# Later stores and weight loads, a fourth evacuation buffer, and a mask added later, in a hybrid decoder layer

## The chip, the cores and the metric

The kernel runs on one core of a Trainium2 chip. The metric is the device time of one execution in microseconds (us). All times below are us unless ns is written.

## What is computed

One layer of a hybrid decoder trunk on a sequence of 1024 rows of 1024 channels, in float32. The rows are normalised, multiplied by one wide input matrix (`w_in`), and the columns of the product feed four mixers of 256 channels each. Cut to what matters here:

```python
h = rms_norm(x, norm_w[i])
c = split_columns(h @ w_in[i])
y_nsa  = nsa_mixer(...)        # sparse attention: compressed, selected and window branch
y_diff = diff_mixer(...)       # differential attention
y_ret  = retention_mixer(...)  # chunked recurrence, chunks of 128 rows
y_ssm  = ssd_mixer(...)        # chunked state-space scan, chunks of 128 rows
# each times silu of a gate column group, concatenated, @ w_out, + x, final rms_norm
```

In the scan (`ssd_mixer`) every chunk needs, for each head, the matrix `exp(cs_l - cs_s)` under a causal mask, multiplied elementwise by the product of C and B, and then products with the rows of x scaled by `dt`.

## The kernel before

Float32 products are made from two parts, a rounded high part and the rest as a low part, so each logical matmul of a projection is three matmuls: high by high, low by high, high by low (L266 to L268 where the weights are stationary, L282 to L284 where the activations are).

Three streams are traced as Python generators and merged by weights: `attention` (differential heads 0 to 3, then sparse heads 4 to 7), `recurrent` (the compression network, then 16 chunks: eight for each pair of heads, of the scan `ssd_group` and of the retention `ret_pair`, zipped), and `projections` (25 groups of weight columns, two more being traced before the merge; then the gates, the output products and the final norm). A scheduler then writes the order of each engine's instructions at build time, from their priorities and a model of their times; attention and recurrence are lifted by 500 places. On the chip an engine takes its list strictly from the head, and so does SP, which issues nearly all DMAs. An edge called NOSYNC binds only the order in that list: on the chip nothing waits for it.

A projection (`proj_t`, or `proj_n` with 256 columns) first loads its weights raw (`weights`, L249, two buffers `wraw`), rounds them on ScalarE (ACT, L253, `whi`), and subtracts on GpSimd (POOL, L186 through `low`, `wlo`). It accumulates in two PSUM banks `mm` over eight steps k, for two halves u of the rows, and an evacuation function per kind of column moves each half through ring `ev` (three buffers of 2 KB a partition) and stores it to DRAM, since the mixers read it in another layout: `evac_split` (two tiles, two stores through `move`, L298), `evac_conv` (convolution and SiLU on VectorE (DVE), store at L752), `evac_rqk`, `evac_rv`, `evac_cmp`, `evac_z`, `evac_zs`. Names put into the set `done` let another stream go on, once its inputs are stored. The ring `ev` also holds the gate rows that `gated` loads back (L1135) and multiplies (DVE, L1136), and the residual rows of `out_partial`.

In `ssd_group` a chunk goes like this: load of x, B, C (`ch`, L761), transposes and the product of B and C (L764 to L766), copy to `xb` (ACT, L768), rows scaled twice on POOL (L771, L772), two loads of the cumulative sums from `d_cs` spread over all partitions (L774 `seg`, L775 `csl`), the causal mask added to `csl` on POOL (L776), per head a sum on DVE (L779) and an exponential on ACT (L781), one product on DVE (L782), and then the matmuls L784, L785 and L787, where L787 needs the result of L782.

Of the kernel before, what the change touches and what calls it, by code (L numbers as in the profile page):

```python
# [11 lines left out]
F32 = mybir.dt.float32  # L12
# [3 lines left out]
ALU = mybir.AluOpType  # L16
# [20 lines left out]
LEAD = 3  # L37
AHEAD = 2
FREE = 8
LO_POOL = 5  # L40
# [82 lines left out]
def hybrid_trunk_kernel(ctx: ExitStack, tc: tile.TileContext, a, out, dbg=None):  # L123
# [5 lines left out]
    dram = ctx.enter_context(tc.tile_pool(name="dr", bufs=1, space=bass.MemoryType.DRAM))  # L129
    RINGS = dict(wraw=(2, 4352), whi=(2, 4352), wlo=(2, 4352), ev=(3, 2048), e=(4, 2048), pth=(3, 2048),  # L130
                 ptl=(3, 2048), t=(8, 1024), u=(4, 1024), sm=(8, 32), sj=(2, 576), ch=(3, 1536), ce=(3, 1024))
# [56 lines left out]
    def bc(ap, n):  # L188

        return ap[:, :, None].to_broadcast([ap.shape[0], ap.shape[1], n])  # L190
# [44 lines left out]


    w_in = a["w_in"][0].rearrange("(k p) c -> p k c", p=P)
    w_out = a["w_out"][0].rearrange("(k p) c -> p k c", p=P)

    def weights(w, cols):  # L240

        c = sum(n for _, n in cols)
        step = 8 if c <= 128 else 4
        parts = []
        for k0 in range(0, NK, step):
            raw = sb("wraw", [P, step, c])
            o = 0
            for off, n in cols:
                SP.dma_start(raw[:, :, o:o + n], w[:, k0:k0 + step, off:off + n])  # L249
                o += n  # L250
            hi = sb("whi", [P, step, c], F32R)
            lo = sb("wlo", [P, step, c], F32R)
            A.activation(hi, raw, AF.Copy)  # L253
            flat = [t_.rearrange("p k c -> p (k c)") for t_ in (lo, raw, hi)]
            low(*flat)
            parts.append((hi, lo))
        return [(parts[k // step][0][:, k % step, :], parts[k // step][1][:, k % step, :]) for k in range(NK)]

    def proj_t(cols, evac):

        w = weights(w_in, cols)
        for u in range(2):
            hs = slice(u * 512, u * 512 + 512)
            p = ps("mm", [P, 512])
            for k in range(NK):
                paced(T.matmul(p, w[k][0], h_hi[k][:, hs], start=(k == 0), stop=False))  # L266
                T.matmul(p, w[k][1], h_hi[k][:, hs], start=False, stop=False)  # L267
                T.matmul(p, w[k][0], h_lo[k][:, hs], start=False, stop=(k == NK - 1))  # L268
                if k < NK - 1:
                    yield  # L270
            evac(u, p)
            yield

    def proj_n(cols, evac, w=None, step=True):

        c = sum(n for _, n in cols)
        w = w or weights(w_in, cols)
        for t in range(NT):
            hs = slice(t * P, (t + 1) * P)
            p = ps("mm", [P, c])  # L280
            for k in range(NK):
                paced(T.matmul(p, h_hi[k][:, hs], w[k][0], start=(k == 0), stop=False))  # L282
                T.matmul(p, h_hi[k][:, hs], w[k][1], start=False, stop=False)  # L283
                T.matmul(p, h_lo[k][:, hs], w[k][0], start=False, stop=(k == NK - 1))  # L284
                if step and k % 2 and k < NK - 1:
                    yield
            evac(t, p)
            yield
# [8 lines left out]
    def move(dst, src):  # L297
        SP.dma_start(dst.bitcast(F32), src.bitcast(F32))  # L298
# [118 lines left out]
    def evac_split(store, j, scale=1.0):  # L417

        def f(u, p):
            hi, lo = sb("ev", [P, 512], F32R), sb("ev", [P, 512], F32R)  # L420
            split(hi, lo, p, scale)
            for i, e in enumerate((hi, lo)):
                move(store[i, j * P:(j + 1) * P, u * 512:u * 512 + 512], e)
        return f
# [310 lines left out]
    def evac_conv(i):  # L735
        tl = const("tl%d" % i, [P, 3])

        def f(u, p):
# [12 lines left out]
            V.scalar_tensor_tensor(acc, th, 1.0, acc, op0=ALU.add, op1=ALU.mult)  # L751
            SP.dma_start(d_conv[i, :, u * 512:u * 512 + 512], acc)  # L752
        return f

    def ssd_group(g):
        dt, da, dd = dtt[:, 0, :], dtt[:, 1, :], dtt[:, 2, :]
        for c in range(NT):
# [46 lines left out]
    def evac_rqk(i, j):  # L804
        def f(u, p):
            e = sb("ev", [P, 512])
            A.activation(e, p, AF.Copy)
            SP.dma_start(d_rqk[i, j, :, u * 512:u * 512 + 512], e)
        return f

    def evac_rv(t, p):
        e = sb("ev", [P, 256])
        A.activation(e, p, AF.Copy)
        SP.dma_start(d_rv[t * P:(t + 1) * P, :], e)

# [93 lines left out]
    def evac_cmp(u, p):  # L909
        ev = sb("ev", [P, 512])  # L910
        A.activation(ev, p, AF.Copy)
        SP.dma_start(d_kv[:, u * 512:u * 512 + 512], ev)

# [210 lines left out]
    def evac_z(ct):  # L1124
        def f(u, p):
            th = sb("ev", [P, 512])
            A.activation(th, p, AF.Tanh, scale=0.5)
            V.scalar_tensor_tensor(th, th, 1.0, p, op0=ALU.add, op1=ALU.mult)
            SP.dma_start(d_z[ct, :, u * 512:u * 512 + 512], th)
        return f  # L1130
# [14 lines left out]
    def evac_zs(t, p):  # L1145
        th = sb("ev", [P, 256])
        A.activation(th, p, AF.Tanh, scale=0.5)
        V.scalar_tensor_tensor(th, th, 1.0, p, op0=ALU.add, op1=ALU.mult)
        SP.dma_start(d_zs[t * P:(t + 1) * P, :], th)

# [137 lines left out]

    done = set()

# [4 lines left out]
    def projections():  # L1295
        run(ssd_prep())
        yield from pt("diff_q", 1, evac_split(d_dq, 1, 32.0 ** -0.5))
        yield from pt("diff_k", 1, evac_split(d_dk, 1))
        done.add("diff1")
# [6 lines left out]
        done.add("nsa")  # L1306
        yield from pt("xbc", 0, evac_conv(0))
# [4 lines left out]
        yield from proj_n([(OFF["ret_v"], 256)], evac_rv)  # L1312
        done.update(("conv0", "ret0"))
        yield from pt("xbc", 1, evac_conv(1))
# [3 lines left out]
        yield from pt("xbc", 5, evac_conv(5))  # L1318
        done.update(("conv1", "ret1"))
        yield from proj_n([(OFF["ssm_z"], 256)], evac_zs)  # L1320
        done.add("ssm_z")
        for ct, n in ((2, "diff_z"), (4, "ret_z"), (0, "nsa_z")):
            for j in range(2):
                yield from pt(n, j, evac_z(ct + j))
        w_out0 = out_weights(ORDER[0:2], 0)[0]
        free(*h_hi, *h_lo)
# [16 lines left out]
        yield from out_final()  # L1343

    proj = projections()
    done.add("diff0")

# [102 lines left out]
```

## Time and profile before

| | |
|---|---|
| median of 3 executions | 753.74 us (751.43 to 753.95) |
| profiled execution, its own time | 753.33 us |
| its span, first to last instruction | 751.4 us |
| TensorE (PE) busy | 710.7 us, 95% |
| VectorE (DVE) busy | 519.6 us, 69% |
| ScalarE (ACT) busy | 409.6 us, 55% |
| GpSimd (POOL) busy | 298.1 us, 40% |
| DMA engines | 105.96 MB, mean 141 GB/s |

The span is shorter than the execution's own time by 1.9 us, which lies around it. A busy share is a mean over stages: idle time of an engine matters only where PE ends up waiting for it.

### The profile page before, as it was taken

How to read it: one execution, taken by the hardware profiler on the slowest of the kernel's cores; microseconds unless marked ns; L12 is line 12 of the kernel's file. 1: busy time of each engine (PE TensorE's matmuls, PEld its weight loads, DVE VectorE, ACT ScalarE, POOL GpSimd, SP SyncE). 2: the span in 40 equal slices, each digit the busy share in tenths (PEclk: the TensorE clock that was granted, in tenths of full speed). 3: DMA queues.
4: the chain of work that ended last, by engine and by line, in shares of the span. 5: the costliest groups of instructions: out<-in, count | busy, mean ns of one | idle time of the engine just before them, and what ended most of it. 6: DMA issues, size and time to landing. Idle time of an engine off the chain costs nothing.

```text
span 751.4 us, 12303 instructions
## 1 busy us (share of the span) xinstructions
PE 710.7 (95%) x3796; PEld 587.6 (78%) x3796; DVE 519.6 (69%) x1493; ACT 409.6 (55%) x1022; POOL 298.1 (40%) x469
## 2 busy tenths in 40 slices
PE   4999999999999999989999999999989999999994
PEld 4988787768888898777899788688766878788773
DVE  4853466446976867778798957667789996345577
ACT  6722465556777656556575544554465853543343
POOL 4233128212132114442533544545577742632522
PEclk9999999999999999999999999999997999999998
DMA  8658826756722533536333723335374233431365
GB/s 295 186 156 240 225 85 179 209 164 178 204 73 89 142 102 92 129 87 179 106 101 98 188 87 84 91 102 134 104 206 127 68 102 129 140 126 60 126 252 196
DMA packets 103406, 105.96 MB, mean 141 GB/s; under 512 B 15747, under 2 KB 78797, under 8 KB 103325
## 3 DMA queue, kind: packets, MB, share of 16 engines
q1 hardware_dynamic: 103244, 104.82, 47.5%
q8 instruction: 30, 0.49, 0.3%
q14 instruction: 36, 0.29, 0.2%
q0 software_dynamic: 96, 0.36, 0.1%
HBM read 72.96 MB, written 32.54 MB: 140 GB/s over the span
## 4 chain that ended last, share of the span: by engine, by line
PE 68%; DVE 14%; DMA 8%; ACT 4%; issue 3%; POOL 2%; SPq 1%; POOLq 0%; DVEq 0%; ACTq 0%
PE mm L266 9%; PE mm L268 9%; PE mm L267 9%; PE S L172 7%; PE O L1106 3%; PE mm L282 3%; PE mm L283 3%; PE mm L284 3%; PE S L1087 2%; DMA t<-d_cs 2%; PE R L1211 1%; PE R L1212 1%; PE R L1213 1%; PE mm L1211 1%; PE S L1031 1%
## 5 line engine op out<-in xcount | busy, mean ns | idle before, releaser
L186 POOL TENSOR_TENSOR wlo<-wraw,whi 128x256 fp32r<-128x256 f32 x132 | 98.5, 777 | 161.8 <-ACT whi L253 148.4
L266 PE MATMUL mm<-h,whi 128*128 128x512 f32 x400 | 160.0, 401 | 0.8 <-ACT whi L253 0.4
L267 PE MATMUL mm<-h,wlo 128*128 128x512 f32 x400 | 159.2, 399 | 0.0
L268 PE MATMUL mm<-h,whi 128*128 128x512 f32 x400 | 159.1, 398 | 0.0
L476 ACT ACTIVATE S<-S,sj 128x512 f32<-128x512 f32 (+3 forms) x192 | 103.3, 538 | 83.2 <-DVE sj L475 61.1
L172 PE MATMUL S<-b,b 100*128 100x256 f32 (+5 forms) x384 | 133.4, 373 | 6.5 <-ACT e L632 2.7
L475 DVE CUSTOM_DVE_ANT_0 S<-S,mk 128x512 f32<-128x512 f32 (+3 forms) x144 | 70.2, 495 | 39.4 <-PE S L172 18.2
L172 PEld LDWEIGHTS S<-b,b 100*128 100x128 f32 (+1 forms) x384 | 72.5, 193 | 24.9 <-ACT S L476 6.6
L266 PEld LDWEIGHTS mm<-h,whi 128*128 128x128 f32 x400 | 75.9, 190 | 16.3 <-ACT whi L253 0.7
L268 PEld LDWEIGHTS mm<-h,whi 128*128 128x128 f32 x400 | 75.7, 189 | 16.4 <-issue 0.4
L267 PEld LDWEIGHTS mm<-h,wlo 128*128 128x128 f32 x400 | 75.9, 190 | 14.4
L1101 POOL TENSOR_SCALAR pth<-e 128x512 fp32r<-128x512 f32 (+2 forms) x64 | 41.4, 649 | 63.4 <-ACT e L1096 28.8
L1096 ACT ACTIVATE e<-S 128x512 f32<-128x512 f32 (+2 forms) x76 | 40.9, 541 | 31.9 <-PE S L1091 19.7
L1102 DVE TENSOR_TENSOR ptl<-e,pth 128x512 fp32r<-128x512 f32 (+2 forms) x64 | 44.9, 706 | 18.1 <-POOL pth L1101 14.2
L282 PE MATMUL mm<-whi,h 128*128 128x256 f32 (+1 forms) x192 | 55.5, 291 | 1.7 <-DVE ev L744 1.1
L283 PE MATMUL mm<-wlo,h 128*128 128x256 f32 (+1 forms) x192 | 55.5, 291 | 0.1
L284 PE MATMUL mm<-whi,h 128*128 128x256 f32 (+1 forms) x192 | 54.2, 288 | 0.0
L473 DVE TENSOR_REDUCE sj<-S 128x1 f32<-128x512 f32 x48 | 32.5, 683 | 17.0 <-PE S L172 10.4
L632 ACT ACTIVATE e<-S 128x512 f32<-128x512 f32 (+1 forms) x64 | 35.9, 568 | 13.6 <-PE S L172 8.2
L282 PEld LDWEIGHTS mm<-whi,h 128*128 128x128 f32 x192 | 36.7, 192 | 2.8 <-DVE ev L744 1.3
L283 PEld LDWEIGHTS mm<-wlo,h 128*128 128x128 f32 x192 | 36.7, 191 | 1.6 <-POOL wlo L186 0.7
L476 ACT ACTIVATION_READ_ACCUMULATOR S<-S,sj 128x1 f32 x192 | 37.6, 196 | 0.0
(321 smaller groups left out, 1652.5 us busy)
## 6 DMA issues: line engine op xcount, KB each, us to landing
wraw<-in_w_in_dram SPq DMA_DIRECT2D x27, 512.0 KB
b<-in_x_dram SPq DMA_DIRECT2D x8, 512.0 KB
t<-d_cs SPq DMA_DIRECT2D x32, 128.0 KB
wraw<-in_w_out_dram SPq DMA_DIRECT2D x16, 256.0 KB
ev<-in_x_dram SPq DMA_DIRECT2D x16, 256.0 KB
d_part<-ev SPq DMA_DIRECT2D x16, 256.0 KB
b<-d_part SPq DMA_DIRECT2D x8, 512.0 KB
out_dram<-b SPq DMA_DIRECT2D x16, 256.0 KB
```

The source lines that it names most:

```text
L172: ins = T.matmul(tile_, *args, **kw)
L186: G.tensor_tensor(dst[:, cs], src[:, cs], hi[:, cs].bitcast(F32), op=ALU.subtract)
L266: paced(T.matmul(p, w[k][0], h_hi[k][:, hs], start=(k == 0), stop=False))
L267: T.matmul(p, w[k][1], h_hi[k][:, hs], start=False, stop=False)
L268: T.matmul(p, w[k][0], h_lo[k][:, hs], start=False, stop=(k == NK - 1))
L282: paced(T.matmul(p, h_hi[k][:, hs], w[k][0], start=(k == 0), stop=False))
L283: T.matmul(p, h_hi[k][:, hs], w[k][1], start=False, stop=False)
L284: T.matmul(p, h_lo[k][:, hs], w[k][0], start=False, stop=(k == NK - 1))
L475: V.tensor_tensor_reduce(s, s, bound, -1.0, -NEG, ALU.add, ALU.min, nm)
L476: A.activation(s, s, AF.Exp, bias=nm, scale=1.0 if bound is None else -1.0, accum_out=self.d[:, b, i, c:c + 1])
L1101: G.tensor_scalar(hl[0], e, 1.0, 1.0, op0=ALU.mult, op1=ALU.mult)
L1102: V.tensor_tensor(hl[1], e, hl[0].bitcast(F32), op=ALU.subtract)
```

## The change

A store of an evacuated projection half is no longer issued where the evacuation is traced: `later` puts it on a list, and `tick`, called after every step k of a projection (every second one in `proj_n`), traces it three steps later, with an edge that puts it behind that step's matmul in the schedule. `mark` does the same with the names in `done`; `flush` traces what is left at the ends. The stores of `evac_n1` and `evac_nsa_v` stay where they were. A load of raw weights gets an edge to the matmul that ended the first half of the projection two before it (`halfway[-2]`). Ring `ev` has four buffers in place of three. In `ssd_group` the addition of the mask (L776 before) gets an edge that puts it behind the second row scaling (L772 before); both are on POOL.

```diff
+DEFER = 3
-    RINGS = dict(..., ev=(3, 2048), ...)
+    RINGS = dict(..., ev=(4, 2048), ...)
+    def later(dst, src):
+        deferred.append([lambda: SP.dma_start(dst, src), DEFER])
+
+    def tick(ins):
+        for d in deferred:
+            d[1] -= 1
+        while deferred and deferred[0][1] <= 0:
+            st = deferred.pop(0)[0]()
+            if st is not None:
+                tc.add_manual_dep(st.ins, ins.ins.name, NOSYNC, reason="later")
+
+    def mark(*names):
+        deferred.append([lambda: done.update(names), DEFER])
+
+    def flush():
+        while deferred:
+            deferred.pop(0)[0]()
...
-                SP.dma_start(raw[:, :, o:o + n], w[:, k0:k0 + step, off:off + n])
+                ins = SP.dma_start(raw[:, :, o:o + n], w[:, k0:k0 + step, off:off + n])
+                if len(halfway) > 2:
+                    tc.add_manual_dep(ins.ins, halfway[-2].ins.name, NOSYNC, reason="raw")
...
-                T.matmul(p, w[k][0], h_lo[k][:, hs], start=False, stop=(k == NK - 1))
+                ins = T.matmul(p, w[k][0], h_lo[k][:, hs], start=False, stop=(k == NK - 1))
+                tick(ins)
...
+            if u == 0:
+                halfway.append(ins)
...
-            SP.dma_start(d_conv[i, :, u * 512:u * 512 + 512], acc)
+            later(d_conv[i, :, u * 512:u * 512 + 512], acc)
...
-            G.tensor_tensor(xs[:, 1], xn, bc(dd[:, hc], 64), op=ALU.mult)
+            scaled = G.tensor_tensor(xs[:, 1], xn, bc(dd[:, hc], 64), op=ALU.mult)
...
-            G.tensor_tensor(csl, csl, pair(m_causal_t), op=ALU.add)
+            ins = G.tensor_tensor(csl, csl, pair(m_causal_t), op=ALU.add)
+            tc.add_manual_dep(ins.ins, scaled.ins.name, NOSYNC, reason="order")
...
-        done.add("cmp")
+        mark("cmp")
```

The other evacuation stores and the other names go through `later` and `mark` in the same way.

## Rows read from the trace of the kernel before

**Rows 1.** Page: busy us (share of the span) xinstructions of each engine.

```profile
PE 710.7 (95%) x3796; PEld 587.6 (78%) x3796; DVE 519.6 (69%) x1493; ACT 409.6 (55%) x1022; POOL 298.1 (40%) x469
```

**Rows 2.** Windows: stretch, length, busy of PE PEld DVE ACT POOL, clock, DMA.

```profile
25.00:725.00 700.00, 680.24 (x3637) 562.15 (x3638) 484.42 (x1413) 381.02 (x954) 279.66 (x440) 0.99 0.46 133
50.00:75.00 25.00, 25.00 (x112) 20.22 (x111) 11.29 (x33) 4.57 (x7) 7.00 (x10) 1.00 0.85 253
322.80:326.15 3.35, 3.35 (x9) 2.61 (x9) 3.23 (x11) 3.32 (x8) 1.57 (x4) 0.50 0.17 65
554.90:558.25 3.35, 3.35 (x12) 2.68 (x12) 3.25 (x13) 2.42 (x6) 2.37 (x4) 0.50 0.97 288
565.20:575.30 10.10, 9.99 (x29) 6.40 (x28) 10.07 (x29) 5.53 (x15) 7.48 (x11) 0.50 0.39 127
```

**Rows 3.** Waits of PE: who ended them, us in total, times, longest.

```profile
PE S L172 <- ACT e L632: 2.7, 1, 2.7
PE O L1106 <- POOL pth L1101: 2.5, 3, 1.4
...
PE S L172 <- ACT e L1096: 1.1, 1, 1.1
```

**Rows 4.** Waits of the other engines.

```profile
POOL t L776 <- DMA t<-d_cs: 39.5, 9, 16.8
DVE t L779 <- POOL t L776: 26.6, 13, 4.4
...
DVE ev L1136 <- DMA ev<-d_z: 7.4, 4, 2.6
```

**Rows 5.** Timelines of SP, POOL, DVE, ACT, PE, third chunk: start, us, instruction, [idle before].

```profile
310.51 0.33 SPq L752 DMA_DIRECT2D d_conv<-ev  x1
...
313.57 0.38 SPq L775 DMA_DIRECT2D t<-d_cs  x1
...
319.04 0.67 POOL L776 TENSOR_TENSOR t<-t,mk 128x256 f32<-128x256 f32 x1 [4.34 <-DMA d_ssm<-t]
...
319.74 0.93 DVE L779 SCALAR_TENSOR_TENSOR t<-t,ncs,t 128x128 f32<-128x128 f32 x2 [4.44 <-POOL t L776]
...
320.30 0.81 ACT L781 ACTIVATE t<-t,ncs 128x128 f32<-128x128 f32 x2 [4.25 <-DVE t L779]
...
321.64 0.44 PE L172 MATMUL S<-b,b 100*128 100x384 f32 x1 [2.66 <-ACT e L632]
```

**Rows 6.** Timelines of POOL and PE, two later chunks.

```profile
476.01 0.67 POOL L776 TENSOR_TENSOR t<-t,mk 128x256 f32<-128x256 f32 x1 [2.93 <-DMA d_ssm<-t]
...
525.67 0.67 POOL L776 TENSOR_TENSOR t<-t,mk 128x256 f32<-128x256 f32 x1 [5.13 <-DMA t<-d_cs]
...
527.37 0.50 PE L1106 MATMUL O<-pth,b 128*128 128x512 f32 x1 [1.38 <-POOL pth L1101]
```

**Rows 7.** Timelines of DVE and PE around the gates.

```profile
550.31 0.75 DVE L1136 SCALAR_TENSOR_TENSOR ev<-b,wret,ev 128x512 f32<-128x512 f32 x1 [2.65 <-DMA ev<-d_z]
...
554.04 0.39 PE L1068 MATMUL O<-ptl,vvc 128*128 128x256 f32 x1 [1.41 <-DVE ptl L293]
```

**Rows 8.** Waits of SP, the DMA queue.

```profile
SPq L249 <- POOL wlo L186: 35.5, 17, 4.8
```

**Rows 9.** Timelines of POOL, DVE and PE: end of the third chunk.

```profile
324.70 0.40 POOL L772 TENSOR_TENSOR t<-t,dtt 128x128 f32<-128x128 f32 x1
...
325.07 0.42 DVE L782 TENSOR_TENSOR t<-t,t 128x256 f32<-128x256 f32 x1
...
327.34 0.56 PE L787 MATMUL R<-t,t 128*128 128x64 f32 x4
```

**Rows 10.** A load of raw weights: SP, and DMA traffic in a window.

```profile
242.07 0.38 SPq L249 DMA_DIRECT2D wraw<-in_w_in_dram  x1
...
245.50:247.00 1.50, 1.50 (x8) 1.24 (x7) 1.43 (x4) 0.42 (x2) 0.00 (x0) 1.00 0.00 0
```

**Rows 11.** POOL: one operation's shortest, median and longest ns.

```profile
L1101 POOL TENSOR_SCALAR pth<-e x64: 396/617/1586, 426.2 to 721.7; 128x512 fp32r<-128x512 f32 x40, 128x384 fp32r<-128x384 f32 x16, 128x256 fp32r<-128x256 f32 x8
```

More of the change, by code (lines that the diff above doesn't have):

```diff
@@ L129, in hybrid_trunk_kernel @@
     dram = ctx.enter_context(tc.tile_pool(name="dr", bufs=1, space=bass.MemoryType.DRAM))
-    RINGS = dict(wraw=(2, 4352), whi=(2, 4352), wlo=(2, 4352), ev=(3, 2048), e=(4, 2048), pth=(3, 2048),
+    RINGS = dict(wraw=(2, 4352), whi=(2, 4352), wlo=(2, 4352), ev=(4, 2048), e=(4, 2048), pth=(3, 2048),
                  ptl=(3, 2048), t=(8, 1024), u=(4, 1024), sm=(8, 32), sj=(2, 576), ch=(3, 1536), ce=(3, 1024))
@@ L234, in hybrid_trunk_kernel @@
     h_lo = [sb("h", [P, S], F32R) for _ in range(NK)]
+    done = set()
+    deferred = []
+    def later(dst, src):
[12 more added lines that the diff above has]
+            deferred.pop(0)[0]()
     w_in = a["w_in"][0].rearrange("(k p) c -> p k c", p=P)
     w_out = a["w_out"][0].rearrange("(k p) c -> p k c", p=P)
+    halfway = []
     def weights(w, cols):
@@ L283, in proj_n @@
                 T.matmul(p, h_hi[k][:, hs], w[k][1], start=False, stop=False)
-                T.matmul(p, h_lo[k][:, hs], w[k][0], start=False, stop=(k == NK - 1))
+                ins = T.matmul(p, h_lo[k][:, hs], w[k][0], start=False, stop=(k == NK - 1))
+                if k % 2:
+                    tick(ins)
                 if step and k % 2 and k < NK - 1:
                     yield
+            if t == HT - 1:
+                halfway.append(ins)
             evac(t, p)
@@ L422, in f @@
             for i, e in enumerate((hi, lo)):
-                move(store[i, j * P:(j + 1) * P, u * 512:u * 512 + 512], e)
+                later(store[i, j * P:(j + 1) * P, u * 512:u * 512 + 512].bitcast(F32), e.bitcast(F32))
         return f
@@ L807, in f @@
             A.activation(e, p, AF.Copy)
-            SP.dma_start(d_rqk[i, j, :, u * 512:u * 512 + 512], e)
+            later(d_rqk[i, j, :, u * 512:u * 512 + 512], e)
         return f
@@ L813, in evac_rv @@
         A.activation(e, p, AF.Copy)
-        SP.dma_start(d_rv[t * P:(t + 1) * P, :], e)
+        later(d_rv[t * P:(t + 1) * P, :], e)
     sbd = const("sbd", [P, P])
@@ L911, in evac_cmp @@
         A.activation(ev, p, AF.Copy)
-        SP.dma_start(d_kv[:, u * 512:u * 512 + 512], ev)
+        later(d_kv[:, u * 512:u * 512 + 512], ev)
     k1cz, k2cz = const("k1c", [P, 3, 64], F32R), const("k2c", [P, 3, 64], F32R)
@@ L1128, in f @@
             V.scalar_tensor_tensor(th, th, 1.0, p, op0=ALU.add, op1=ALU.mult)
-            SP.dma_start(d_z[ct, :, u * 512:u * 512 + 512], th)
+            later(d_z[ct, :, u * 512:u * 512 + 512], th)
         return f
@@ L1148, in evac_zs @@
         V.scalar_tensor_tensor(th, th, 1.0, p, op0=ALU.add, op1=ALU.mult)
-        SP.dma_start(d_zs[t * P:(t + 1) * P, :], th)
+        later(d_zs[t * P:(t + 1) * P, :], th)
     def ssm_rows(u):
@@ L1287, in hybrid_trunk_kernel @@
     V.tensor_scalar(lam[:, 2:3], lam[:, 2:3], -LAM_INIT, None, op0=ALU.add)
-    done = set()
     wret = const("wret", [P, 4])
@@ L1298, in projections @@
         yield from pt("diff_k", 1, evac_split(d_dk, 1))
-        done.add("diff1")
+        mark("diff1")
         yield from proj_t([(OFF["k_cmp"], 128)], evac_cmp)
-        done.add("cmp")
+        mark("cmp")
         yield from proj_t([(OFF["k_slc"], 64), (OFF["k_win"], 64)], evac_split(d_nk, 0))
@@ L1305, in projections @@
         yield from pt("nsa_q", 1, evac_split(d_nq, 1, 0.125))
-        done.add("nsa")
+        mark("nsa")
         yield from pt("xbc", 0, evac_conv(0))
@@ L1312, in projections @@
         yield from proj_n([(OFF["ret_v"], 256)], evac_rv)
-        done.update(("conv0", "ret0"))
+        mark("conv0", "ret0")
         yield from pt("xbc", 1, evac_conv(1))
@@ L1318, in projections @@
         yield from pt("xbc", 5, evac_conv(5))
-        done.update(("conv1", "ret1"))
+        mark("conv1", "ret1")
         yield from proj_n([(OFF["ssm_z"], 256)], evac_zs)
-        done.add("ssm_z")
+        mark("ssm_z")
         for ct, n in ((2, "diff_z"), (4, "ret_z"), (0, "nsa_z")):
@@ L1324, in projections @@
                 yield from pt(n, j, evac_z(ct + j))
+        flush()
         w_out0 = out_weights(ORDER[0:2], 0)[0]
@@ L1343, in projections @@
         yield from out_final()
+    flush()
     proj = projections()
```

## Prediction

> **What bounds the kernel now.** I read the page first: PE is busy 710.7 of 751.4 us [rows 1], so the most that any reordering can give is 40.7 us. The windows divide this: from 25 to 725 us PE is idle 700 - 680.2 = 19.8 us [rows 2]; the other 20.9 us lie in the head, where the inputs land, and in the tail, where the last norm is stored, and no edit touches either. Beside the idle time there is the clock. It is granted in full nearly everywhere, but in three stretches of the windows it stands at 0.5, the 1.2 GHz level: 3.35 us at 322.8, 3.35 us at 554.9 and 10.1 us at 565.2 [rows 2]. The dense window at 50 us passes 112 matmuls in 25 us, 0.223 us each [rows 2]; in 3.35 us that would be 15, and in 10.1 us 45. What went through was 9, 12 and 29, so the three stretches lost 6, 3 and 16 matmuls, an estimate of 1.3, 0.7 and 3.6 us.
>
> The third view is PE's own waits. Few are long: one of 2.7 us for an exponential of ACT, three of 2.5 us together for a tile of POOL, one of 1.1 us for ACT [rows 3]. They name the engine that was last, not the cause. The waits of the other engines tell that: POOL stood 39.5 us in nine waits at the mask addition L776 for the loads of `d_cs`, and DVE stood 26.6 us at L779 for POOL [rows 4].
>
> The timeline of the third chunk shows the whole mechanism. SP issues a store of a convolved projection at 310.51, when its data are ready, and the load of `csl`, queued behind it, only at 313.57. POOL reaches the mask addition and stands 4.34 us, until 319.04 (the view blames a store, but the addition reads `csl`, issued 5.5 us earlier). DVE stands 4.44 us at L779, ACT 4.25 us at L781, and an exponential of the attention queued behind on ACT frees PE's bank late: PE is idle 2.66 us until 321.64 [rows 5]. The clock falls 1.2 us later, at 322.8 [rows 2]. The same addition ends POOL's waits at 476.01 and 525.67 (2.93 and 5.13 us), and PE waits 1.1 us for ACT after the first [rows 3, 6] and 1.38 us for a tile of POOL after the second [rows 6]. So a load that is late by some us reaches PE through three engines whose lists are strict.
>
> A fourth stall is of another kind. At 550.31 DVE had waited 2.65 us for gate rows in a buffer of ring `ev`, and PE then waited 1.41 us for a DVE result, until 554.04 [rows 7]; the half clock at 554.9 follows [rows 2].
>
> **The mask edge.** It adds no instruction: 16 additions of 0.67 us [rows 5] move from ahead of the row scaling to behind it on POOL. In the third chunk the addition ran at 319.04 and the second scaling at 324.70 [rows 5, 9], so `csl` gets 5.7 us more to land, against a wait of 4.34. Queued behind the addition on POOL in the old order were, among others, the tiles that PE waited for; they no longer wait for this load. What goes: 2.66 + 1.3 us of clock at 319, 1.1 at 477, 1.4 at 526, together 6.5 us.
>
> What it costs: before, the decay matrix was ready when the scaled rows were; now it begins after them. From the start of the second scaling to the products L787 it took 327.34 - 324.70 = 2.64 us [rows 9]. Now one after another: scaling 0.40, addition 0.67, two sums 0.93, the second exponential 0.40, product 0.42 [rows 5, 9], 2.82 us and four hand-overs of up to 0.1 us, so 3.2 us at most. This is 0.6 us more in a chunk. No PE wait at a chunk's product stands in rows 3 or among the longer ones, so the low bound is nothing; the high bound is that PE stands for all of it in all 16 chunks, 9.6 us. I take 1 us, near the low end, since PE's list has projection matmuls to place between. Whether a chunk later in the recurrence matters: the additions of the tenth and the thirteenth stand at 476.01 and 525.67 [rows 6], 16.6 us a chunk, of which the piece that grows is 2.64, so the cover is large.
>
> **Stores asked for later.** The SP list loses waits at its head, and the loads behind come sooner, as between 310.51 and 313.57 [rows 5]. These loads are what the mask addition waits for, so this gain is the same as above and is not counted twice. The stores themselves land three steps later, 3 x 3 x 0.223 = 2.0 us of matmuls; the readers are gated by `mark` in the same way. I take nothing for it, covered by the projections that run between a store and its reader; without that cover it would be 2 us at each of the six calls of `mark`, 12 us in all, if the reader were what PE waits for.
>
> **Raw weights asked for later.** SP stood 35.5 us in 17 waits at L249, for POOL to free the raw buffer [rows 8]; half a projection later the buffer is long free. The loads behind these get up to 4.8 us. The price is slack: the load issued at 242.07 had no traffic left after 245.5, so it took at most 3.4 us [rows 10]. A projection has 48 matmuls, 10.7 us at 0.223, and the load now comes half a projection, 5.4 us, before ACT may round it. So 2 us remain in the densest stretch, more where attention is interleaved. I take nothing for either side.
>
> **A fourth buffer.** Each deferred tile is held some 2 us longer, and one buffer more carries that. Where `ev` serves the gates, one load more can be under way: DVE waited 7.4 us in four waits there [rows 4]. I take the 1.4 us stall and its 0.7 us of clock, 2.1 us; low bound nothing, if the buffer is spent on something else.
>
> **The sum.** 6.5 + 2.1 - 1.0 = 7.6 us. The profiled execution took 753.33, 1.9 us more than its span and 0.4 under the median shown: 753.33 - 7.6 = 745.7 us. The half clock at 565 is left in, since DVE is busy 10.07 of its 10.1 us [rows 2] and a full clock could not be used.
>
> **A rule against it.** POOL's 617 ns tile took up to 1586 ns in places [rows 11], with DVE at work beside it. The Trainium skill, in "SBUF — State Buffer", section "SBUF: two separate sides", has the two share a port pair as an exclusive lock, held for a whole instruction by a GpSimd operation or a DVE operation with two SBUF inputs. By that rule an addition moved from idle time into busy time blocks DVE or is blocked; the trace agrees that durations stretch, and by it the sum would come out at rival two below. By the rows alone it stays 745.7.
>
> **The rivals.**
> One, no change: the stalls come back elsewhere. Either the 9.6 us of the longer chunk fall on PE, 753.3 - 8.6 + 9.6 = 754.3, or the lists, written anew, put other instructions at the head that wait. Seven stalls of the size in rows 3 (1.1 each) eat the gain. For it: DVE has 10.07 of 10.1 us at 565. Against: loads, whose time varies most, leave the heads of three lists. 0.20.
>
> Two, POOL and DVE get in each other's way: 16 additions of 0.67 us each hold up one DVE instruction, at worst 10.7 us, but DVE is full only around 550 to 600 and PE waits for it mostly there; I put 6 us on PE, 745.7 + 6 = 751.7. The Trainium skill's rule above says the same. For this rival speak the 1586 ns of rows 11; against it, that DVE is idle 31% of the span [rows 1]. 0.06.
>
> Three, slower: raw loads come late. If a load takes longer than the 5.4 us that half a projection leaves, ACT stands at L253 with attention's exponentials queued behind, and PE waits for its banks as in rows 5. It decides from 0.7 us of PE at each of the 17 loads that SP had to hold back before [rows 8]: 17 x 0.7 = 11.9 us, 745.7 + 11.9 = 757.6, and with 1.2 us each 766. For it: DMA is 0.85 busy at 50 us [rows 2] and a chunk's loads took 5.5 us [rows 5]. Against: 3.4 us in rows 10. 0.16.
>
> Four, more gain: with SP free, the work around 550 to 575 is spread out, and the 3.6 us of clock go too, with a third of the 13.2 us of idle time that the four stalls leave in place (19.8 - 2.7 - 1.1 - 1.4 - 1.4): 745.7 - 3.6 - 4.4 = 737.7. Against it: DVE is full there whatever SP does. 0.12.
>
> That the change does nothing is not likely: the order of the addition alone is certain to differ. It is within rival one.
>
> **How the numbers follow.** My forecast, 741.5 to 749.5, gets 0.46. A difference of 0.5%, 3.8 us, is about what a measurement of this kernel can tell from none: faster is below 750, slower above 757.5. Faster: forecast and rival four, 0.58. Same: rivals one and two, 0.26. Slower: rival three, 0.16. The range goes from rival four's 737.5 to 757, which leaves out most of rival three and little below; the likeliest alone has 741.5 to 749.5.
>
> **What would show it.** In the profile after: POOL's waits at the mask addition for `d_cs` fall from 39.5 us to under 5; ACT and DVE stand less at L781 and L779; SP's waits at the raw loads vanish; PE shows no 2.7 us wait and full clock around 320; DVE waits less for gate rows; idle PE between 25 and 725 falls from 19.8 to about 14. Wrong would be: waits of ACT at the rounding for `wraw`, new waits of PE at L787 for the product, a longer half clock after 550, or the recurrence ending well after 600.

## The result, and the profile after

The changed kernel took 743.64 us, median of four executions (742.82 to 745.74), against 753.85 (751.43 to 754.33) for the kernel before, measured beside it: a ratio of 0.9875, with a 95% interval of 0.9846 to 0.9905. Run once more, beside later experiments, it took 743.61, a ratio of 0.9815 (0.978 to 0.985). It is faster; the forecast was 745.7 in a range of 737.5 to 757. The profiled execution took 743.5 for a span of 741.6, 9.8 us less than before.

The page of the kernel after, the row that answers to [rows 1]:

```profile
PE 706.1 (95%) x3796; PEld 589.8 (80%) x3796; DVE 516.7 (70%) x1493; ACT 410.8 (55%) x1022; POOL 300.4 (41%) x469
```

Windows of the kernel after (columns as in [rows 2]):

```profile
25.00:725.00 700.00, 685.94 (x3683) 572.49 (x3682) 491.20 (x1432) 388.41 (x972) 284.21 (x443) 0.99 0.46 137
...
300.00:540.00 240.00, 236.02 (x1352) 203.19 (x1350) 180.00 (x557) 132.68 (x330) 118.21 (x198) 0.99 0.44 124
540.00:610.00 70.00, 63.79 (x347) 52.46 (x347) 64.45 (x195) 45.53 (x134) 48.45 (x71) 0.88 0.39 121
610.00:725.00 115.00, 114.43 (x564) 93.05 (x563) 68.02 (x150) 50.61 (x120) 43.49 (x59) 1.00 0.39 135
584.60:741.60 157.00, 145.18 (x725) 117.33 (x724) 102.74 (x238) 71.83 (x183) 61.62 (x80) 0.98 0.40 139
...
541.30:558.40 17.10, 13.88 (x54) 11.77 (x55) 16.59 (x53) 8.80 (x29) 12.96 (x22) 0.50 0.77 249
```

The same stretches in the kernel before, the last from its own last store of retention to its end:

```profile
300.00:540.00 240.00, 231.06 (x1306) 194.56 (x1306) 179.07 (x554) 129.00 (x329) 110.77 (x192) 0.99 0.42 113
540.00:610.00 70.00, 65.77 (x361) 53.31 (x359) 63.27 (x175) 43.84 (x122) 51.26 (x75) 0.90 0.45 138
610.00:725.00 115.00, 111.44 (x551) 89.54 (x550) 65.49 (x158) 50.32 (x120) 42.96 (x59) 1.00 0.36 121
600.40:751.40 151.00, 136.87 (x674) 110.17 (x673) 96.70 (x224) 65.42 (x161) 57.38 (x75) 0.98 0.40 141
```

Idle time of PE between 25 and 725 fell from 19.8 to 14.1 us. From 300 to 540, where most of the chunks run, it is 8.9 us before and 4.0 after. From 540 to 610 it is the other way round, 4.2 before and 6.2 after, and the half clock there is now one stretch of 17.1 us. From 610 to 725 it is 3.6 before and 0.6 after. A stretch of equal time also holds more work after: from 300 to 540 PE passed 1352 matmuls in place of 1306. The last store of retention was issued at 600.4 before and at 584.6 after, 15.8 us sooner. (Tile `d_ret`, the kernel before and then the kernel after; the last number of the start column is the last issue:)

```profile
L867 SPq DMA_DIRECT2D d_ret<-u x16: 319/332/448, 312.7 to 600.4; - x16
```

```profile
L903 SPq DMA_DIRECT2D d_ret<-u x16: 319/326/528, 310.7 to 584.6; - x16
```

These 15.8 us are not a gain of which 6 were lost again: behind that store PE still had 725 matmuls to pass after, and 674 before. The recurrence got ahead of the other streams, and more of their work now stands behind it.

The split of the gain into idle and busy time of PE is not steady. Of the 9.8 us of span, 5.2 are idle time (40.7 to 35.5) and 4.6 are busy time, for the same 3796 matmuls. Profiled once more, the changed kernel had a span of 741.4 us, nearly the same, but from 540 to 610 a clock of 0.95 and 10.3 us idle, in place of 0.88 and 6.2:

```profile
540.00:610.00 70.00, 59.71 (x348) 48.93 (x347) 62.89 (x194) 44.95 (x133) 47.77 (x71) 0.95 0.39 120
```

So differences of a few us of idle time in that stretch tell nothing by themselves. From 300 to 540 the two profiles agree (4.0 and 3.6).

The waits of the kernel after, PE first, then POOL, DVE and SP (lines have moved: the mask addition is L811, the first sum L815, the raw load L275, a deferred store L243):

```profile
PE S L1030 <- DMA b<-d_nq: 3.0, 1, 3.0
...
PE R L799 <- issue: 2.7, 2, 2.5
...
POOL t L811 <- DMA t<-d_cs: 0.4, 1, 0.4
...
DVE ev L1172 <- DMA ev<-d_z: 7.2, 3, 3.4
...
DVE t L815 <- POOL t L811: 5.8, 5, 2.8
...
SPq L243 <- ACT ev L326: 22.8, 8, 7.3
...
SPq L275 <- POOL wlo L187: 4.8, 3, 3.3
```

POOL's wait of 39.5 us at the addition for `d_cs` [rows 4] has become 0.4 us, and DVE's behind it went from 26.6 to 5.8. (16.8 of the 39.5 were a single wait, at the first addition, at 181.87; PE's idle time from 25 to 300 is 3.0 us before and 3.3 after, so nothing came back there.) PE's longest wait of the middle, 2.7 us for an exponential [rows 3], is gone; a load of `d_nq` takes 3.0 us in its place. SP's 35.5 us at the raw loads [rows 8] are 4.8. DVE's wait for gate rows has not fallen (7.4 to 7.2).

Nor did the deferral free SP. At the stores of the high parts in `evac_split` it stood 22.8 us in 8 waits for ACT (L243). Before, with the store at L298, and in the kernel below that has the stores back where they were, it is the same row within 2 us (the kernel before, then that one):

```profile
SPq L298 <- ACT ev L291: 21.2, 8, 7.1
```

```profile
SPq L243 <- ACT ev L326: 22.4, 8, 7.3
```

What the edge does is seen on SP and POOL, third chunk, kernel after (timeline as in [rows 5]):

```profile
313.13 0.54 SPq L810 DMA_DIRECT2D t<-d_cs  x1
...
318.90 0.40 POOL L806 TENSOR_TENSOR t<-t,dtt 128x128 f32<-128x128 f32 x1 [0.48 <-ACT t L803]
319.26 0.40 POOL L807 TENSOR_TENSOR t<-t,dtt 128x128 f32<-128x128 f32 x1
319.62 0.68 POOL L811 TENSOR_TENSOR t<-t,mk 128x256 f32<-128x256 f32 x1
```

The load is issued at much the same time as before (313.57 [rows 5]), and the addition runs at 319.62, no sooner than before (319.04). What comes sooner is the work that stood behind it: the second row scaling is at 319.26 instead of 324.70 [rows 9]. Before, the scaling waited for ACT's copy `xb`, and that copy stood in ACT's list behind the exponential (L781) that the late addition held until 320.30 [rows 5] (kernel before, POOL and ACT):

```profile
323.75 0.48 ACT L768 ACTIVATE t<-R 128x384 f32<-128x384 f32 x1
...
324.30 0.44 POOL L771 TENSOR_TENSOR t<-t,dtt 128x128 f32<-128x128 f32 x1 [3.78 <-ACT t L768]
```

So the whole chunk is some 5 us ahead, though PE's listed stall there was 2.66 us.

### The profile page after: what moved, and what is told of

Its sections match the earlier page's. It is cut to its first block, busy times and chain, and to the rows that moved or that the text cites. A ratio compares the mean times of both kernels' runs of the same rounds, so it can differ in the third digit from the quotient of the medians.

```text
span 741.6 us, 12307 instructions
## 1 busy us (share of the span) xinstructions
PE 706.1 (95%) x3796; PEld 589.8 (80%) x3796; DVE 516.7 (70%) x1493; ACT 410.8 (55%) x1022; POOL 300.4 (41%) x469
## 4 chain that ended last, share of the span: by engine, by line
PE 82%; DVE 7%; DMA 7%; ACT 1%; issue 1%; POOL 1%; SPq 0%; POOLq 0%; DVEq 0%; ACTq 0%
PE mm L294 12%; PE mm L295 12%; PE mm L296 12%; PE S L173 9%; PE O L1142 4%; PE mm L313 3%; PE mm L314 3%; PE mm L315 3%; DMA b<-in_x_dram 2%; PE S L1123 2%; PE R L1247 2%; PE R L1248 2%; PE R L1249 2%; PE S L1067 1%; PE mm L1247 1%; PE mm L1249 1%
## 5 line engine op out<-in xcount | busy, mean ns | idle before, releaser
L173 PE MATMUL S<-b,b 100*128 100x256 f32 (+5 forms) x384 | 129.9, 364 | 2.7 <-ACT S L511 2.5
L510 DVE CUSTOM_DVE_ANT_0 S<-S,mk 128x512 f32<-128x512 f32 (+3 forms) x144 | 70.6, 496 | 45.1 <-PE S L173 19.8
L1138 DVE TENSOR_TENSOR ptl<-e,pth 128x512 fp32r<-128x512 f32 (+2 forms) x64 | 46.6, 735 | 20.4 <-POOL pth L1137 17.1
L232 POOL TENSOR_TENSOR sm<-sm,mhalf 128x2 f32<-128x2 f32 (+3 forms) x30 | 25.5, 852 | 35.5 <-DVE sm L231 29.2
```

Of the source, the lines that this page charges most:

```text
L173: ins = T.matmul(tile_, *args, **kw)
L510: V.tensor_tensor_reduce(s, s, bound, -1.0, -NEG, ALU.add, ALU.min, nm)
L1138: V.tensor_tensor(hl[1], e, hl[0].bitcast(F32), op=ALU.subtract)
```

## The experiments

The theory after the result: the mask edge alone makes the gain, because a load that lands late at the head of POOL's list holds POOL, DVE and ACT, and PE behind them. The rivals: the later stores, the raw loads or the buffer make it; or lists that are written anew come out faster by chance. A third theory, tried with an earlier load and with a late one, is that the addition's place in the lists counts, and not the late load.

All twelve runs are in one table, beside the kernel before and the changed one, so that each can be read against the rest. The ratio is to the kernel before on the same chip, in interleaved rounds; the next columns are of the profiled execution: DVE's wait for the addition (in the two runs with a ring `cs`, including the load itself where it is named), PE's idle time from 300 to 540 and from 540 to 610, and the last store of retention. The two rows of the changed kernel show how far the idle time of one kernel scatters.

| kernel | us | ratio (95%) | DVE's wait | idle 300 to 540 | idle 540 to 610 | last `d_ret` |
|---|---|---|---|---|---|---|
| before | | 1 | 26.6 | 8.9 | 4.2 | 600.4 |
| changed | 743.64 | 0.9875 (0.9846 to 0.9905) | 5.8 | 4.0 | 6.2 | 584.6 |
| mask edge alone | 742.63 | 0.9804 (0.978 to 0.9828) | 6.5 | 1.5 | 9.0 | 586.7 |
| changed, without the mask edge | 763.06 | 1.0067 (1.004 to 1.0093) | 39.6 | 15.3 | 7.4 | 609.7 |
| changed, stores where they were | 741.27 | 0.9789 (0.9765 to 0.9814) | 7.1 | 2.1 | 8.4 | 588.6 |
| lists rewritten, nothing changed | 755.68 | 0.9993 (0.9971 to 1.0015) | 28.1 | 11.6 | 7.5 | 602.5 |
| changed, again | 743.61 | 0.9815 (0.978 to 0.985) | 5.3 | 3.6 | 10.3 | 584.4 |
| ring of its own, no edge | 757.06 | 1.0019 (0.9989 to 1.0048) | 17.0 | 4.2 | 5.6 | 598.2 |
| ring of its own and edge | 750.67 | 0.9906 (0.9869 to 0.9943) | 3.7 | 0.5 | 8.0 | 597.2 |
| later stores alone | 761.41 | 1.0067 (1.0036 to 1.0097) | 37.6 | 12.7 | 8.1 | 613.4 |
| edge, load late again | 756.47 | 1.0007 (0.9982 to 1.0031) | 15.2 | 3.4 | 9.1 | 595.9 |
| stores back, edges in retention | 751.85 | 0.9936 (0.991 to 0.9961) | 4.5 | 4.3 | 13.0 | 599.2 |
| four buffers alone | 760.57 | 1.0061 (1.0038 to 1.0084) | 35.0 | 8.8 | 9.8 | 607.8 |
| later raw loads alone | 757.13 | 1.0017 (0.9991 to 1.0044) | 28.7 | 9.8 | 6.3 | 605.3 |

**The mask edge alone**, on the kernel before:

```diff
+            scaled = G.tensor_tensor(xs[:, 1], xn, bc(dd[:, hc], 64), op=ALU.mult)
...
+            tc.add_manual_dep(ins.ins, scaled.ins.name, NOSYNC, reason="order")
```

> The kernel before with the mask edge alone. Theory (the prediction's largest term): POOL's waits at the mask addition for the loads of d_cs fall from 39.5 us to under 5, DVE's wait for POOL at the sums from 26.6 to under 10, and the time falls by about 5.5 us (6.5 less 1 for the longer chunk), ratio 0.993. Rival A (the SP queue brings the gain, by stores and raw loads asked for later): the waits fall but the time by less than 2 us. Rival B (the lists are written anew, and the time of any new set of lists scatters): the time moves either way by up to 5 us, with PE's stalls in new places.

It has the whole gain. Its windows and its wait of DVE:

```profile
300.00:540.00 240.00, 238.54 (x1371) 204.99 (x1371) 185.06 (x582) 135.63 (x341) 117.60 (x201) 0.99 0.44 121
540.00:610.00 70.00, 61.04 (x334) 48.21 (x333) 63.35 (x178) 44.19 (x127) 47.10 (x68) 0.93 0.38 117
...
DVE t L780 <- POOL t L776: 6.5, 4, 2.7
```

**Everything but the mask edge**: the changed kernel with that edge taken out.

```diff
-            tc.add_manual_dep(ins.ins, scaled.ins.name, NOSYNC, reason="order")
```

> The changed kernel without the mask edge: stores later, raw loads later, four buffers. Theory: about 2 us under the kernel before (751 to 752), with POOL's waits at the mask addition still above 25 us, some less than 39.5 since the loads leave SP sooner. Rival A: these waits fall to under 15 us because SP is free, and most of the 10 us gain stays (744 to 746). Rival B: any time between 744 and 756.

The rest of the change costs time, and the waits at the addition are all there and longer (waits of POOL, DVE and ACT in that kernel):

```profile
POOL t L811 <- DMA t<-d_cs: 37.5, 7, 17.1
...
DVE t L814 <- POOL t L811: 39.6, 14, 5.6
...
ACT t L816 <- DVE t L814: 42.5, 16, 5.4
```

**The changed kernel with the stores and names where they were**; mask edge, raw loads and four buffers stay.

```diff
     def later(dst, src):
-        deferred.append([lambda: SP.dma_start(dst, src), DEFER])
+        SP.dma_start(dst, src)
...
     def mark(*names):
-        deferred.append([lambda: done.update(names), DEFER])
+        done.update(names)
```

> The changed kernel with the stores and the names in done where they were; mask edge, raw edge and four buffers stay. Theory: the deferral is worth nothing by itself, 743 to 746. Rival A: it carries part of the gain, 748 or more, and SP's waits at stores are back. Rival B: anywhere from 740 to 752.

With the mask edge in, the stores' place makes no difference that the intervals show (0.9789 against 0.9815 in the second run of the changed kernel, on another chip; the intervals overlap). The first ratio of the changed kernel, 0.9875 (0.9846 to 0.9905), would put them apart, but its time is the same as in the second, 743.6 us: what differs is the kernel before that was measured beside it (753.85 and 755.39). On one chip with the edge alone this kernel took 741.27 us against 742.63, so the raw loads and the buffer cost nothing that shows once the edge is in.

**A control**: the kernel before with one weight of the merge changed, so that the lists of all engines are written anew about as much as by the change.

```diff
-W_ATT, W_REC, W_PROJ = 400, 70, 660
+W_ATT, W_REC, W_PROJ = 400, 70, 655
```

> A control: the kernel before with the merge weight of the projections 655 in place of 660, none of the edits. It rewrites the lists as much as the change does and aims at nothing. Theory: within 3 us of the kernel before, with POOL's waits at the mask addition still 30 us or more. Rival B: 4 us or more away, up or down, which would put the whole gain within reach of accident.

The time stays, and so do the waits (DVE 28.1). That lists written anew gain 2% by chance is not borne out by this draw, nor by the other five kernels of the table that have no mask edge, each with lists of its own: they lie at 1.0017 to 1.0067, and none is faster than before. With the edge the kernels lie at 0.9789 to 1.0007, so what else stands in the lists decides how much of its gain is left.

**The changed kernel again**, beside the next ones on their chip, with no edit:

> The changed kernel itself, measured again beside the others on one chip. Theory now: the mask edge alone makes the gain and the deferral of stores costs a little, so this is some 1 to 3 us over the kernel with the mask edge alone, ratio to the kernel before 0.981 to 0.988.

It took 1.0 us more than the kernel with the edge alone, on another chip, and its ratio, 0.9815, lies in the range expected.

**An earlier load instead of a later reader.** The kernel before with `seg` and `csl` in a ring of their own, so that their loads need not wait for a buffer of the chunk before; once without and once with the mask edge:

```diff
-                 ptl=(3, 2048), t=(8, 1024), u=(4, 1024), ...
+                 ptl=(3, 2048), t=(6, 1024), cs=(4, 1024), u=(4, 1024), ...
-            seg, csl = sb("t", [P, 2, P]), sb("t", [P, 2, P])
+            seg, csl = sb("cs", [P, 2, P]), sb("cs", [P, 2, P])
```

> The kernel before, with seg and csl in a ring of their own (four buffers of 1 KB; ring t gets six in place of eight), so that their loads need not wait for the products of the chunk before; the mask addition stays ahead of the row scaling, no other edit. Theory (it is the late load at POOL's head that reaches PE): POOL's waits at the mask addition fall to under 10 us and most of the gain comes without the mask edge, 743 to 748. Rival C (it is the place of the addition and of the sums and exponentials behind it in the lists of DVE and ACT): the waits fall likewise, but the time stays within 3 us of the kernel before.

> The kernel before with both the mask edge and the ring of their own for seg and csl. Theory: the load is then late for nobody, the two cures overlap, and it is within 2 us of the mask edge alone. Rival C: no different from the mask edge alone either, so this run tells mostly whether anything of the load's lateness was left.

Both expectations missed. Without the edge the kernel took 757.06 us in place of 743 to 748, and the waits at the addition only halve, 19.7 us in place of under 10, with 14.7 us more of DVE for the loads themselves: the addition moves ahead in the lists as its load does. PE's idle time from 300 to 540 did fall, to 4.2 us. With the edge it took 750.67 us, 8.0 more than the edge alone, in place of within 2. The line of the addition in the kernel without the edge, and what POOL waited for there:

```profile
L776 POOL TENSOR_TENSOR cs<-cs,mk x16: 671/674/908, 89.7 to 525.3; 128x256 f32<-128x256 f32 x16
...
  DMA cs<-d_cs: 19.7, 8
```

The first addition now stands at 89.7 us; in the kernel before the recurrence's additions begin at 181.9. Both kernels lose time near 90 us, in the dense stage: PE's idle time from 25 to 300 is 6.5 and 7.7 us in them against 3.0 before. The timeline of the one with the edge shows how:

```profile
85.95 1.88 SPq L774 DMA_DIRECT2D cs<-d_cs  x1
...
88.82 0.43 SPq L775 DMA_DIRECT2D cs<-d_cs  x1
89.35 0.85 SPq L298 DMA_DIRECT2D d_dq<-ev  x2
...
94.59 0.69 DVE L293 TENSOR_TENSOR ev<-mm,ev 128x512 fp32r<-128x512 f32 x1 [4.41 <-DMA d_dq<-ev]
...
96.87 0.50 PE L172 MATMUL S<-b,b 100*128 100x512 f32 x1 [3.15 <-ACT S L476]
```

Four loads stand on SP ahead of a store, though with the edge the first mask addition runs at 297.7. The store's buffer of `ev` is free late, DVE waits 4.41 us for it and PE 3.15 us behind. In the kernel with the edge alone the same instruction of DVE, at 88.86, waits for no store, only 1.40 us for ACT. Whether the store was late for its place on SP or for the transfers of these loads is not parted: from 84 to 92 us the DMA engines were busy all the time in both kernels (1.00, and 1.01 with the edge alone). A load can be asked for too early as well as too late.

**The later stores alone**, with three buffers, raw loads and addition as before:

> The kernel before with the stores and names asked for later, three buffers, no other edit. Theory: no gain or a loss, 753 to 762, with POOL's waits at the mask addition still over 30 us; SP's waits for evacuations shrink little, since the edge binds only the list. Rival A (SP is freed): under 751.

It costs 0.67% (0.36 to 0.97), and DVE's wait at the addition rises from 26.6 to 37.6. SP's row at the stores of the high parts is 20.8 us in 8 waits, 21.2 before: as expected, the deferral hardly changes when SP gets to a store. What in these lists costs the time is not settled.

**The mask edge, and the load late again**: a second edge asks for the load of `csl` only behind the row scaling too.

```diff
-            SP.dma_start(csl, d_cs[1:2, hc, :].to_broadcast([P, 2, P]))
+            ld = SP.dma_start(csl, d_cs[1:2, hc, :].to_broadcast([P, 2, P]))
+            tc.add_manual_dep(ld.ins, scaled.ins.name, NOSYNC, reason="late")
```

> The kernel before with the edge on the mask addition, as in the run with that edge alone (742.6 us), and with a second edge: the load of the mask's rows is asked for only behind the same row product, so that it lands late again, about 2 us after it is issued by the list, while the addition still stands behind the row product in GpSimd's list. Theory T (what counted was that a load landed after its reader had come to the head of GpSimd's queue): GpSimd's waits for d_cs come back, some 20 to 40 us in sum, ScalarE and VectorE wait for it at the next two steps, and the time goes back to 748 to 756 us. Rival C (what counted was only the place of the addition in the list, among other work of GpSimd): waits of less than 10 us in sum and 741 to 745 us.

The time is back at that of the kernel before, 0.5 us above the range of theory T, and the waits are back in small pieces, just under its range: 18.3 us in eleven, none over 2.8. One of them, in the timeline, with its way through the engines:

```profile
533.07 0.42 SPq L775 DMA_DIRECT2D t<-d_cs  x1
...
537.28 0.67 POOL L777 TENSOR_TENSOR t<-t,mk 128x256 f32<-128x256 f32 x1 [2.79 <-DMA t<-d_cs]
537.91 1.27 POOL L1101 TENSOR_TENSOR ptl<-e,pth 128x512 fp32r<-128x512 f32 x1
...
537.98 1.60 DVE L781 SCALAR_TENSOR_TENSOR t<-t,ncs,t 128x128 f32<-128x128 f32 x2 [3.21 <-POOL t L777]
...
539.36 0.69 ACT L783 ACTIVATE t<-t,ncs 128x128 f32<-128x128 f32 x2 [5.37 <-DVE t L781]
...
539.23 0.39 PE L1108 MATMUL O<-ptl,b 128*128 128x256 f32 x1 [0.76 <-POOL ptl L1101]
...
540.97 0.66 PE L789 MATMUL R<-t,t 128*128 128x64 f32 x4 [0.72 <-DVE t L784]
```

From its issue to the start of its reader 4.2 us pass, where about 2 were expected. This late load reaches PE: 0.76 us for a tile that stood behind the addition on POOL, and 0.72 us for the chunk's product. But most of the additions that wait stand ahead of it, and from 300 to 540 PE is idle 3.4 us, much nearer to the 1.5 of the mask edge alone than to the 8.9 before. The loss comes after 540: 9.1 us idle, about as with the edge alone (9.0), but at a clock of 0.88 in place of 0.93 to 610, and half clock again around 615. PE's longer stalls there, 1.19 us until 544.97 and 2.87 until 548.27, wait for ACT and DVE; that they follow from the same load is not shown. So this run does not part the two theories: by its total and its waits it is near what the late-load theory says, by the stretch from 300 to 540 it is mostly as the place in the list says.

**The same kind of edge at retention**, on the changed kernel with the stores back. POOL still waited 12.0 and 9.9 us for these loads in the changed kernel; with the stores back only the second wait is there, 10.0 us:

```diff
+            cp = A.activation(kv[:, 0, :], p1[:, 2, :], AF.Copy)
...
+            for i_ in (i1, i2):
+                tc.add_manual_dep(i_.ins, cp.ins.name, NOSYNC, reason="order")
```

> The changed kernel with the stores where they were before, as in the run of 741.3 us, and the same kind of edge at a second place: GpSimd's two products of the retention stage that read loads (the zeta product and the xi product) stand behind ScalarE's copy of k in the lists. Theory T (a reader of a load at the head of GpSimd's queue holds the engines behind it): GpSimd's waits for d_rqk and d_rv, 12.0 and 9.9 us in the changed kernel, fall under 5 us each; if PE lost time behind them the run is 1 to 5 us faster, 736 to 740 us. Rival C (retention's waits are covered by other work): the waits fall and the time stays at 740 to 744 us.

No wait of POOL for either load is left, and the kernel is slower than without these edges, which neither theory expected: 751.85 us, 0.9936 against 0.9789, on another chip, and the intervals lie far apart. The timeline shows PE's longest new stall:

```profile
551.04 1.68 DVE L1196 SCALAR_TENSOR_TENSOR h<-h,h 128x1024 f32<-128x1024 f32 x1 [3.19 <-DMA h<-d_zs]
...
554.95 0.42 DVE L328 TENSOR_TENSOR ptl<-S,pth 128x256 fp32r<-128x256 f32 x1
...
555.42 0.58 PE L1106 MATMUL O<-ptl,vvc 128*128 128x256 f32 x1 [5.50 <-DVE ptl L328]
```

In the lists written with these edges, a DVE instruction that reads a load of `d_zs` stands at the head of DVE's list 3.19 us before the load lands; the attention's tile is queued behind it and other work, and PE stands 5.50 us, its longest wait outside the head. It is the pattern of [rows 5] with another load, on another engine. The late load itself is not new: without these edges the same instruction waited 1.7 us for its other load, `d_ssm`, and with the mask edge alone 2.28 us for `d_zs`. What differs is what stands behind it.

**Four buffers alone, and the later raw loads alone**, each on the kernel before (the lines are those of the change):

> The kernel before with four evacuation buffers in place of three and nothing else. The forecast's term: 2.1 us less (a ratio of 0.997), and VectorE's waits for d_z at the gate rows fall from 7.4 us. Rival C (the waits at the gate rows are for the load and not for a buffer): the waits stay at 6 to 10 us and the ratio is 0.999 to 1.002.

> The kernel before with the loads of raw weights asked for later and nothing else. The forecast's term: nothing, a ratio of 0.998 to 1.002, with SyncE's waits at the raw loads (35.5 us in 17) gone. Rival three of the forecast (a raw load lands after its rounding wants it): ScalarE or GpSimd wait for the raw weights by more than 3 us in sum and the ratio is 1.005 or more.

The kernel with the buffer alone is 0.61% slower (0.38 to 0.84). DVE's wait for gate rows went from 7.4 only to 6.2, as rival C had it, though the ratio is outside what either side expected, and its wait at the addition rose from 26.6 to 35.0. The raw loads alone do nothing: SP's waits for POOL there fell from 35.5 to 9.2, ACT waited for no raw load at the rounding of a projection (2.5 us in two at the output's weights, 2.4 before), POOL for none at the subtraction (the one row of POOL that names a raw load, 2.8 us, is at the mask addition), and the interval holds 1.

## Why the prediction was right, and where it was not

**The total was right, through two errors of opposite sign.** The mask edge was put at 6.5 - 1.0 = 5.5 us. Alone it gave 1.72% to 2.20% in interleaved rounds, on 753.33 us 13 to 17, and 8.7 us between the two profiled executions (751.4 - 742.7). The rest of the change was put at a gain of 2.1. Without the mask edge it costs 0.40% to 0.93%, 3 to 7 us; with it, no cost shows. So the hit on the total is luck in part, while the mechanism of its largest term, the late load that holds three engines, is borne out by the edge alone.

**The step that failed for the edge** is "what goes: 2.66 + 1.3 us of clock at 319, 1.1 at 477, 1.4 at 526". It counted the waits that PE's view listed behind three of the sixteen additions. But a chunk's addition also held the row scaling of its own chunk (324.70 before, 319.26 after), so the recurrence got late without PE standing still just there. That PE took other work meanwhile and lacked it later is an inference. What the runs show is the sum: with the edge alone PE's idle time from 300 to 540 fell from 8.9 to 1.5, 7.5 us against the 5.2 of idle time that the forecast had listed there, it passed 1371 matmuls in that stretch in place of 1306, and the recurrence ends 13.7 us sooner. Over the whole span the idle time fell by 3.8 us and the busy time by 4.9. Why the rounds show more than the traces is not settled; the kernel before took 753.4 to 760.06 on that chip, its profiled execution is at the low end, and the profiled execution with the edge, 744.55, is the slowest of its four.

**A reading that was wrong** in the same part: `csl` does not get "5.7 us more to land". The second scaling stood at 324.70 only because the wait had made it late too. With the edge the addition runs 0.6 us later than before; the wait is gone because POOL has its other work done by then.

**The price of the half clock** was low. It counted matmuls of different sizes as equal. In the trace after, matmuls of 512 columns start 0.43 us apart at the half clock and 0.23 at full (the lines are in the last section). By that a stretch in which PE is always busy loses nearly half its length, an estimate of 1.6 us for each of the stretches of 3.35 us (in place of 1.3 and 0.7) and 4.7 for the one of 10.1 (in place of 3.6).

**The edge's cost**, 1.0 us for a longer chunk, is not to be seen: PE waits at the products L823 for 0.2 us in all in the trace after, and the branch of rival one that made it 9.6 is out.

**The fourth buffer**, 2.1 us of gain, is the term that was wrong in sign. It was tied to DVE's wait for gate rows; that stayed at 7.2 in the changed kernel and at 6.2 with the buffer alone. With four buffers SP still waited for one at the load of these rows (L1135): 7.6 us until POOL had read it, 6.0 before. Whether the 0.61% are the buffer's or those of lists written anew was not parted.

**The later stores** were put at nothing. In the changed kernel that holds; alone they cost 0.36% to 0.97%. The working had SP lose waits at its head, so that the loads behind come sooner. That step failed: SP stood at the stores of the high parts 22.8 us in 8 waits for ACT, against 21.2 in 8 before, and in the third chunk the load of `csl` left SP only 0.4 us sooner (313.13, before 313.57). In each of the kernels that lose without the mask edge, DVE's wait at the addition is longer than before (35.0, 37.6, 39.6), and with the edge there is no loss that shows: this fits a cost that reaches PE through the same late addition. It was not tried by itself.

**The raw loads** at nothing: as forecast, and rival three (late raw loads) did not come about.

**Rival two**, POOL and DVE in each other's way: the sixteen moved additions took 674 ns in the median after, 671 before, and none over 718, and DVE's busy time did not rise (519.6 to 516.7 us). In the run with the edge alone one took 1652 ns, at 546.42, beside a DVE product of two tiles that ran from 546.07 to 547.54. The Trainium skill's rule of the exclusive lock ("SBUF — State Buffer", section "SBUF: two separate sides") may stand behind that one; it did not set the time, since that run has the whole gain.

**What was said to be wrong signs.** One appeared: the half clock after 550 came at 541.3 and is longer, 17.1 us against 3.35 and 10.1 before [rows 2]. DVE is busy there 16.59 of 17.1 us and the DMA engines 0.77; that the recurrence, now ahead, meets the gates and the output's loads there is a likely reading, not a tested one. No cost of it shows in the total: the second profile of this kernel has a clock of 0.95 from 540 to 610 and a span of 741.4 us, against 0.88 and 741.6. This is as the forecast said of the half clock at 565: where DVE is full, a full clock gave no gain. The idle time of 14.1 us between 25 and 725, as forecast ("about 14"), is luck: the second profile of the same kernel has 17.8.

**What stays open**: how much of the edge's gain is the late load and how much the place of the addition among POOL's other work. An early load alone kept half of the waits, and a late load with the edge kept most of the gain up to 540 but lost it after. And the stretch from 540 to 610 comes out differently in each of these kernels, 4.2 to 13.0 us idle, and 6.2 and 10.3 in two profiles of one; a few of its stalls were traced to a late load, the others were not settled.

## What to carry to other kernels

Look for the instruction that waits longest for a load at the head of a strict list, and put work that is ready ahead of it, rather than asking for the load sooner: here one edge gave what the whole change gave. Price such a wait by what is queued behind it on every engine it holds, not by PE's listed stalls alone. And measure each part of a change by itself, since here the other parts cost 0.7% by themselves, which did not show beside the good one; edges that took POOL's waits for loads away at another place made the kernel slower, and in the lists written with them another late load held more work behind it.

## What the runs showed of the hardware that was not expected

Loads issued early cost time: four of them, from 85.95 to 88.82 us, stood on SP ahead of a store, and PE stood 3.15 us. And the clock: in the trace after PE stood 3.0 us until 345.62, and from 346.6 to 350.3 the granted clock is 0.54, though PE was busy in all of it; before the long stretch at 541.3 PE had been busy 0.06 us in the one from 539 to 540 and 0.66 in the next, and then the clock stood at 0.50, the 1.2 GHz level, for 17.1 us with PE busy in 13.88 of them. The two windows, and two pairs of matmuls of the same size, at the end of the first window and behind it:

```profile
346.60:350.30 3.70, 3.70 (x16) 3.42 (x16) 1.80 (x7) 1.10 (x5) 0.00 (x0) 0.54 0.04 14
...
539.00:540.00 1.00, 0.06 (x1) 0.00 (x0) 1.00 (x6) 0.92 (x2) 0.21 (x1) 1.00 0.42 125
```

```profile
349.07 0.63 PE L294 MATMUL mm<-h,whi 128*128 128x512 f32 x1
349.50 0.63 PE L295 MATMUL mm<-h,wlo 128*128 128x512 f32 x1
...
350.53 0.39 PE L295 MATMUL mm<-h,wlo 128*128 128x512 f32 x1
350.76 0.39 PE L296 MATMUL mm<-h,whi 128*128 128x512 f32 x1
```

At 0.43 us in place of 0.23 for each such matmul, the 3.7 us lost some 1.7 us, an estimate. So the stall of 3.0 us cost more than its own length here, if the half clock is counted to it. For the stretch of 17.1 us, where DVE was full, no such cost shows.
